# The upper MLP layer of two passes by seven block products of eight, with the weights' block sums made on the side

## The chip, the cores and the metric

The kernel runs on one core of one Trainium2 chip. The metric is the device time of one execution in microseconds (us). The engines are named as in the profile: PE (TensorE matmuls) with PEld (its weight loads), DVE (VectorE), ACT (ScalarE), POOL (GpSimd) and SP (SyncE, which here issues most DMAs).

## The reference

One encoder layer on 2048 tokens of 1024 features, one batch. What matters here is the last third of it:

```python
h = h + concat([att, conv], -1) @ w_out          # mixing: attention and convolution
h = h + cross_attention(rmsnorm(h, norm_x_g)) @ w_xo
u = rmsnorm(h, norm_mlp_g[l]) @ w_up[l]          # 1024 -> 4096, the upper layer
h = h + jnp.square(jax.nn.relu(u)) @ w_down[l]   # 4096 -> 1024, the lower layer
return rmsnorm(h, norm_final_g)
```

Attention is a sliding window at three dilations (8 heads of 64), the convolution has 31 taps over 512 channels. All in float32.

## The kernel before

**Arithmetic.** Every float32 operand of a large product is split into a high and a low float16 part (`split_to`, or an ACT cast and a DVE subtraction), and each product is three matmuls, high by high, high by low, low by high (`mm3`, L370 to L372). A 128x128 block of weights is loaded for every matmul and up to 512 tokens stream past it; sums collect in a PSUM bank of 512 columns.

**Passes.** After the first linear layers the tokens are worked off in four passes `p` of 512 tokens each (`post(p)`). A pass first applies `w_out` (`resid_linear`, tiles `o`), then cross attention (scores `xs`, softmax, output tiles `x` by a second `resid_linear`), then the MLP. Activations are kept with features on the partitions: `hs[m]` is a tile of 128 features by 512 tokens, m from 0 to 7. `resid_linear` makes `hs[m]` on DVE, multiplies it by the norm's gain and splits it into `y["h", m]` and `y["l", m]` (names `mh`, `ml` for the MLP), and adds its square to `ssum`. The norm's factor per token is applied after the product, at the eviction of the upper layer (`rsb`).

**MLP of the first three passes.** The 4096 hidden features are eight groups `fg` of four tiles `c`. For two groups at a time the hidden tiles are made one after the other (tile `up`, 24 matmuls each; then DVE L1601, ACT square L1602, ACT cast L1604, DVE subtraction L1605 give `hhh` and `hhl`), and then eight output tiles (`dn`, 24 matmuls each) add the lower layer's share to `hs[m]` (DVE L1620). Both kinds take turns in three PSUM banks, `mm=(0, 1, 2)`. The lower layer's product runs over the eight hidden tiles in order, k from 0 to 7.

**Weights.** The first pass loads float32 weights, splits them (L357 on ACT, L358 on DVE) and saves the float16 pairs to DRAM tiles `wst`, 512 KB each. The later passes load `wst` again, through a ring of seven tiles (`wtile`, `wpost`). The last pass has its own MLP (`last_mlp`), which already makes its lower layer by seven block products.

**Order of the work.** Python generators yield after each piece. `weave(main, *sides)` runs the pass's generator and, at each of its yields (a main step), lets the side generators advance at a given rate; beside pass p run the attention of pass p+1 (`att`, 0.95) and its convolution (`conv`, 0.85, from main step 23 on in the second and third pass). A convolution step is four DVE instructions on `cacc` (L387). The second pass has 8 steps for `w_out`, 8 for the scores, 11 for the cross attention's output, and 16 for each pair of groups. This is the order in which instructions are written; a list scheduler then fixes each engine's own order by estimated times, taking what stands first and is ready. `issue_after` queues an instruction behind another one of the same engine. Within an engine the order is then fixed. All the weights' DMAs go through SP's queue, in order.

`load_cat` fills the four tiles of the pool `cat0` with the next pass's mixed features late in the MLP, at the last pair of groups.

Of the kernel before, what the change touches and what calls it, by code (L numbers as in the profile page):

```python
# [10 lines left out]
F32 = mybir.dt.float32  # L11
# [10 lines left out]
P = 128  # L22
# [26 lines left out]
def hybrid_layer(ctx, tc, A, out):  # L49
# [69 lines left out]
    wst = [dr.tile([P, 2 * 1024], F16, name=f"wst{i}") for i in range(64)]  # L119
    vscr = dr.tile([P, 2, 8, 256], F16, name="vscr")  # L120
# [25 lines left out]
    gxm = cst.tile([P, 16], F32, name="gxm")  # L146
# [5 lines left out]
    cst.tile([P, 64], F32, name="cpad")  # L152
# [101 lines left out]
    def bounds():  # L254
# [9 lines left out]
        with ExitStack() as st:  # L264
# [13 lines left out]
            TT(c[19], c[0], g2m, op=ALU.mult)  # L278
        yield
# [10 lines left out]
        with ExitStack() as st:  # L290
# [13 lines left out]
            TS(gxm[:, 8:16], gv[:, 16:24], TM, None, op0=ALU.mult)  # L304
        yield
# [1113 lines left out]
    banks.update(mm=(0, 1, 2), O=(7,))  # L1419
# [5 lines left out]
    cv = pool("conv")  # L1425

    def tmp(name, bufs=4, dtype=F32, shape=(P, 512)):
        return pp.tile(list(shape), dtype, tag="tmp", name=name, bufs=bufs)
# [44 lines left out]
    def resid_linear(load, rhs, korder, resid, hs, ssum, scale, gains, y, name, steps=False, wide=False):  # L1473


        for ms in ((0, 1, 2, 3) if wide else (0, 1, 2), () if wide else (3,), (4,), (5,), (6,), (7,)):
# [3 lines left out]
            for ks in [korder[a:b] for a, b in zip(cuts, cuts[1:])] if len(ms) > 1 else (korder,):  # L1480
                for m, (wh, wl) in zip(ms, wt):
# [6 lines left out]
                    if ks[-1] == korder[-1]:  # L1488
# [3 lines left out]
                        ACT.activation(y["h", m], h, AF.Copy, scale=g)  # L1492
                        DVE.scalar_tensor_tensor(y["l", m], h, g, y["h", m], op0=ALU.mult, op1=ALU.subtract)  # L1493
                        add_sq(h, ssum, m == 0)
                        yield

    def post(p):
# [48 lines left out]
        for hp in range(XH // 2):  # L1546
# [4 lines left out]
            for kk in range(4):  # L1551
                ah, al = wpost(ascr[hp, :, 2 * kk:2 * kk + 2, :], f"a{p}{hp}{kk}", S_A, (P, 2, 512))
                for t in range(4):
# [8 lines left out]
                    if kk == 3:  # L1562
# [4 lines left out]
        y = ytiles("m")  # L1567
        ssum = ssum_tile(f"x{p}")
        xl = resid_linear(lambda m: wpost(bscr[m], f"b{p}{m}", S_B), pr_, list(range(KC)), lambda m: hs[m], hs, ssum, K_B,
                          gxm[:, 8:16], y, f"x{p}_", True)  # L1570
# [4 lines left out]
        yield from xl  # L1575
        r = rstd_from(ssum)
        rb = ps("c", "nrb")
        bcast_rows(rb, r, 4)
        rsb = ssum
# [7 lines left out]
        for g in range(FG // 2):  # L1587
            end = g == FG // 2 - 1
            hh = {}
            for fg in (2 * g, 2 * g + 1):  # L1590
                for q in "hl":
                    t = xquad(q, fg % 2, f"hh{q}{p}_{fg}")
                    for j in range(4):
                        hh[q, 4 * (fg % 2) + j] = t[:, j]
                for c in range(4):
                    wh, wl = wpost(wcols(w_up, fg * 512 + c * P), f"u{p}{fg}_{c}", S_UP, (P, 8, P), 4 * fg + c, p)
                    pt = ps("mm", "up")
                    for k in range(KC):
                        mm3(pt, wh[:, k, :], wl[:, k, :], y["h", k], y["l", k], k == 0, k == KC - 1)
# [3 lines left out]
                    j = 4 * (fg % 2) + c  # L1603
# [6 lines left out]
            for mp2 in range(4):  # L1610
                ws = [wpost(wcols(w_down, mp2 * 256, 256, (4 * fg, 4 * fg + 4)), f"d{p}{fg}_{mp2}", S_DN, (P, 4, 256),
                            32 + 4 * fg + mp2, p) for fg in (2 * g, 2 * g + 1)]
                for e in range(2):
# [3 lines left out]
                    for k in range(8):  # L1617
                        wh, wl = ws[k // 4]
                        mm3(pt, wh[:, k % 4, es], wl[:, k % 4, es], hh["h", k], hh["l", k], k == 0, k == 7)
# [178 lines left out]
    for p in range(NG):  # L1798
# [8 lines left out]
        if p + 1 < NG:  # L1807
            cg = conv(cv, p + 1)
            sides = [(att(p + 1), 0.95), (cg, 0.85)]
            weave(islice(main, 23 if p else 14), sides[0])  # L1810
# [60 lines left out]
```

## Time and profile before

| | |
|---|---|
| median of 3 runs | 2701.93 us (2701.36 to 2705.62) |
| profiled execution | 2703.95 us, of which the span from first to last instruction is 2702.1 us |
| instructions | 40538 |
| granted PE clock, mean | 0.994 |
| HBM | 342.52 MB read, 102.12 MB written, 165 GB/s over the span |
| DMA issues of 512 KB for the MLP | `ws_u<-wst` 96, `ws_d<-wst` 64 |

The page gives each engine's busy time, its share of the span in 40 slices, the chain of work that ended last, and the costliest groups of instructions by line, with the mean duration of one and the idle time ahead of them. Views of the trace give the same for a stretch of time, and the waits of an engine with what ended them. Durations of neighbouring instructions on an engine overlap, so that the distance between their starts is the price of one in a stream.

### The profile page before, as it was taken

How to read it: one execution, taken by the hardware profiler on the slowest of the kernel's cores; microseconds unless marked ns; L12 is line 12 of the kernel's file. 1: busy time of each engine (PE TensorE's matmuls, PEld its weight loads, DVE VectorE, ACT ScalarE, POOL GpSimd, SP SyncE). 2: the span in 40 equal slices, each digit the busy share in tenths (PEclk: the TensorE clock that was granted, in tenths of full speed). 3: DMA queues.
4: the chain of work that ended last, by engine and by line, in shares of the span. 5: the costliest groups of instructions: out<-in, count | busy, mean ns of one | idle time of the engine just before them, and what ended most of it. 6: DMA issues, size and time to landing. Idle time of an engine off the chain costs nothing.

```text
span 2702.1 us, 40538 instructions
## 1 busy us (share of the span) xinstructions
PE 2643.7 (98%) x15514; PEld 1447.3 (54%) x15514; DVE 1842.6 (68%) x3565; ACT 1141.9 (42%) x2029; POOL 228.6 (8%) x285
## 2 busy tenths in 40 slices
PE   7989999999899999999999999999999999999998
PEld 7844448777454555445555554455555545444443
DVE  5887656567679996556676763467776435668886
ACT  5737544476454345334531222244221323434433
POOL 1234002032002011100000000000000000000000
PEclk9999999999999999999999999999999999999999
DMA  8977978665635777864344545344445445223231
GB/s 261 300 259 215 285 225 268 171 182 172 169 90 165 235 221 221 259 190 147 113 128 129 147 126 169 123 122 126 135 118 150 148 125 164 94 94 102 89 121 63
DMA packets 396322, 447.31 MB, mean 166 GB/s; under 512 B 87549, under 2 KB 302513, under 8 KB 395360
## 3 DMA queue, kind: packets, MB, share of 16 engines
q1 hardware_dynamic: 388720, 429.70, 53.1%
q10 hardware_dynamic: 5184, 9.01, 0.9%
q0 software_dynamic: 2224, 6.01, 0.6%
q8 instruction: 122, 2.00, 0.3%
q14 instruction: 72, 0.59, 0.1%
HBM read 342.52 MB, written 102.12 MB: 165 GB/s over the span
## 4 chain that ended last, share of the span: by engine, by line
PE 85%; DVE 5%; DMA 5%; ACT 2%; issue 2%; SPq 1%; POOL 0%; DVEq 0%; POOLq 0%; ACTq 0%
PE up L370 8%; PE up L371 8%; PE up L372 8%; PE dn L371 8%; PE dn L370 8%; PE dn L372 8%; PE lin L372 3%; PE lin L371 3%; PE lin L370 3%; PE pt L1026 2%; PE xs L371 2%; PE xs L372 2%; PE o L372 2%; PE xs L370 2%; PE o L370 2%; PE o L371 2%
## 5 line engine op out<-in xcount | busy, mean ns | idle before, releaser
L371 PE MATMUL up<-ml,ws_u 128*128 128x512 f16 x1024 | 388.6, 380 | 0.9 <-DVE ml L1493 0.9
L370 PE MATMUL up<-mh,ws_u 128*128 128x512 f16 x1024 | 388.4, 380 | 0.8 <-DMA ws_u<-wst 0.8
L372 PE MATMUL up<-mh,ws_u 128*128 128x512 f16 x1024 | 387.9, 379 | 0.0
L387 DVE SCALAR_TENSOR_TENSOR cacc<-cu,cw,cacc 128x512 f32<-128x512 f32 x480 | 366.8, 765 | 7.6
L370 PE MATMUL dn<-hhh,ws_d 128*128 128x512 f16 x768 | 290.7, 379 | 0.4 <-ACT hhh L1604 0.4
L371 PE MATMUL dn<-hhl,ws_d 128*128 128x512 f16 x768 | 290.7, 379 | 0.3 <-DVE hhl L1605 0.3
L372 PE MATMUL dn<-hhh,ws_d 128*128 128x512 f16 x768 | 290.7, 379 | 0.0
L1029 ACT CAST ph<-pt 128x512 f16<-128x512 f32 x160 | 91.8, 575 | 217.5 <-PE pt L1026 217.4
L1019 DVE CUSTOM_DVE_ANT_0 sm<-s,mask,qks 128x256 f32<-128x256 f32 (+1 forms) x384 | 150.8, 435 | 46.1 <-PE s L1237 31.5
L1620 DVE SCALAR_TENSOR_TENSOR h<-dn,bd,h 128x512 f32<-128x512 f32 x96 | 71.9, 750 | 152.8 <-PE dn L372 151.2
L372 PEld LDWEIGHTS <-ws_u 128*128 128x128 f16 x1024 | 100.5, 98 | 121.6 <-issue 1.9
L1020 ACT ACTIVATE sm<-sm,o 128x256 f32<-128x256 f32 (+1 forms) x288 | 117.2, 453 | 114.1 <-DVE o L1019 113.7
L370 PEld LDWEIGHTS <-ws_u 128*128 128x128 f16 x1024 | 100.4, 98 | 114.1 <-DMA ws_u<-wst 1.7
L371 PEld LDWEIGHTS <-ws_u 128*128 128x128 f16 x1024 | 100.3, 98 | 112.4 <-issue 0.6
L1030 DVE TENSOR_TENSOR pl<-pt,ph 128x512 f16<-128x512 f32 x160 | 109.9, 687 | 42.7 <-ACT ph L1029 42.5
L1602 ACT ACTIVATE rl<-rl 128x512 f32<-128x512 f32 x96 | 60.0, 627 | 164.0 <-DVE rl L1601 163.8
L1601 DVE SCALAR_TENSOR_TENSOR rl<-up,ssumx 128x512 f32<-128x512 f32 x96 | 65.8, 689 | 92.7 <-PE up L372 91.3
L372 PEld LDWEIGHTS <-ws_d 128*128 128x128 f16 x768 | 75.1, 98 | 90.5 <-issue 0.4
L370 PEld LDWEIGHTS <-ws_d 128*128 128x128 f16 x768 | 75.5, 98 | 83.0
L371 PEld LDWEIGHTS <-ws_d 128*128 128x128 f16 x768 | 75.1, 98 | 83.1
L1026 PE MATMUL pt<-ident,sm 128*128 128x128 f32 x640 | 98.4, 275 | 6.4 <-ACT sm L1020 3.3
L372 PE MATMUL o<-cath,ws_o 128*128 128x512 f16 x256 | 97.7, 383 | 4.3 <-DVE ws_o L358 4.3
(499 smaller groups left out, 6123.9 us busy)
## 6 DMA issues: line engine op xcount, KB each, us to landing
ws_u<-wst SPq DMA_DIRECT2D x96, 512.0 KB
ws_d<-wst SPq DMA_DIRECT2D x64, 512.0 KB
raw_d<-in_w_down_dram SPq DMA_DIRECT2D x36, 512.0 KB
scan<-in_w_up_dram SPq DMA_DIRECT2D x32, 512.0 KB
scan<-in_w_down_dram SPq DMA_DIRECT2D x32, 512.0 KB
raw_o<-in_w_out_dram SPq DMA_DIRECT2D x32, 512.0 KB
raw_a<-ascr SPq DMA_DIRECT2D x32, 512.0 KB
raw_b<-bscr SPq DMA_DIRECT2D x32, 512.0 KB
```

Of the source, the lines that this page charges most:

```text
L370: PE.matmul(o, lh, rh, start=first, stop=False, skip_group_check=more)
L371: PE.matmul(o, lh, rl, start=False, stop=False, skip_group_check=more)
L372: last["pe"] = PE.matmul(o, ll, rh, start=False, stop=end, skip_group_check=more)
L387: DVE.scalar_tensor_tensor(acc, u[:, t:t + 512], cw[:, c, t:t + 1], acc, op0=ALU.mult, op1=ALU.add)
L1019: last["dve"] = DVE.tensor_tensor_reduce(dst, so, mask[:, 256 * m:256 * m + nk], SCORE, 3e38, ALU.add, ALU.min, mn)
L1020: last["act"] = ACT.activation(dst, dst, AF.Exp, bias=mn, scale=-1.0)
L1026: last["pe"] = PE.transpose(pt[:, j, :], sm[:, j, :], ident)
L1029: ACT.copy(ph, pt)
L1030: DVE.tensor_tensor(pl, pt, ph, op=ALU.subtract)
L1601: last["dve"] = DVE.scalar_tensor_tensor(r, pt, 0.0, rsb, op0=ALU.max, op1=ALU.mult)
L1602: ACT.activation(r, r, AF.Square)
L1620: last["dve"] = DVE.scalar_tensor_tensor(hs[m], pt, K_DN, hs[m], op0=ALU.mult, op1=ALU.add)
```

## The change

In the second and third pass (p = 1 and 2) the upper layer of a group `fg` is no longer four tiles of 24 matmuls with 512 columns. The product is taken as 2x2 blocks: the weights' input features in two halves (k 0 to 3, k 4 to 7), the group's hidden features in two halves of two tiles, and the tokens in two halves of 256. Seven products of blocks with sums of blocks replace the eight (`quad`): each is 24 matmuls of 256 columns. Three PSUM banks X, Y and Z hold partial sums; `kept` copies a bank to SBUF by ACT, `done` adds a bank to such a copy on DVE and makes the hidden tiles.

The sums of the activations' blocks (`B11`, `T1`, `T4`, `B2`, `T32`, and `B12` in the second pass) are made where `hs[m]` is made (`put_columns`, in place of the plain split). The sums of the weights' blocks are made by a new side generator (`prep`), twelve steps for a group: it loads the float32 weights into the `cat0` tiles, adds blocks on DVE, splits on ACT and DVE, and stores seven tiles of 512 KB a group to new DRAM tiles `ust`. In the second pass it runs at rate 1.0 from main step 8 on and prepares groups 3 to 7, in the third at 0.6 for groups 0, 1 and 2. So the second pass uses `quad` for groups 3 to 7 only, and makes groups 0 to 2 from the old weights, in two halves of 256 tokens; the third uses it for all eight, in the order 3 to 7, 0 to 2, and issues the first step of its first quad ahead of the norm's sums (`opened`). After quads the lower layer takes k in the order 0, 1, 2, 3, 6, 7, 4, 5. The scale bounds get factors 4 and 16, and `tmp` a fifth buffer. The first and the last pass keep their way.

```diff
@@ buffers and bounds
+    ust = [[dr.tile([P, 2 * 1024], F16, name=f"ust{fg}_{i}") for i in range(7)] for fg in range(8)]
...
+            TS(c[0], c[0], 4.0, None, op0=ALU.mult)
+            TS(c[18], c[18], 16.0, None, op0=ALU.mult)
...
+            TS(gxm[:, 16:24], gxm[:, 8:16], -1.0, None, op0=ALU.mult)
...
-    banks.update(mm=(0, 1, 2), O=(7,))
+    banks.update(mm=(0, 1, 2), ux=(0,), uy=(1,), uz=(2,), O=(7,))
...
-    def tmp(name, bufs=4, dtype=F32, shape=(P, 512)):
+    sw = pool("sums")
+    def tmp(name, bufs=5, dtype=F32, shape=(P, 512)):
@@ resid_linear
-                        ACT.activation(y["h", m], h, AF.Copy, scale=g)
-                        DVE.scalar_tensor_tensor(y["l", m], h, g, y["h", m], op0=ALU.mult, op1=ALU.subtract)
+                        if put:
+                            put(m, h, g)
+                        else:
+                            ACT.activation(y["h", m], h, AF.Copy, scale=g)
+                            DVE.scalar_tensor_tensor(y["l", m], h, g, y["h", m], op0=ALU.mult, op1=ALU.subtract)
@@ new
+    def prep(fgs):
+        late = []
+        def give(d, t):
+            late.append((d, t))
+        def step():
+            for d, t in late:
+                dma(d, t)
+            late.clear()
+        def hi(o, i):
+            ACT.activation(o, i, AF.Copy, scale=S_UP)
+        def lo(o, i, h):
+            DVE.scalar_tensor_tensor(o, i, S_UP, h, op0=ALU.mult, op1=ALU.subtract)
+        for fg in fgs:
+            for j in range(2):
+                nm = f"{fg}{j}"
+                raw = [ct0.tile([P, 8, P], F32, tag=f"ch{i}", name=f"pw{i}_{nm}") for i in range(2)]
+                step()
+                for i in range(2):
+                    dma(raw[i], wcols(w_up, (4 * fg + 2 * i + j) * P))
+                a11, a12, a21, a22 = (r[:, 4 * i:4 * i + 4] for r in raw for i in range(2))
+                yield
+                step()
+                t0 = ct0.tile([P, 2, 8, P], F16, tag="cl0", name=f"pt0_{nm}")
+                hi(t0[:, 0], raw[0])
+                s1 = sw.tile([P, 4, P], F32, tag="s1", name=f"ps1_{nm}")
+                DVE.tensor_tensor(s1, a21, a22, op=ALU.add)
+                DVE.tensor_tensor(a21, a11, a21, op=ALU.subtract)
+                yield
+                step()
+                lo(t0[:, 1], raw[0], t0[:, 0])
+                give(ust[fg][j], flat(t0))
+                DVE.tensor_tensor(a11, s1, a11, op=ALU.subtract)
+                t2 = ct0.tile([P, 2, 8, P], F16, tag="cl1", name=f"pt2_{nm}")
+                hi(t2[:, 0], raw[1])
+                yield
+                step()
+                DVE.tensor_tensor(a12, a12, a11, op=ALU.subtract)
+                lo(t2[:, 1], raw[1], t2[:, 0])
+                give(ust[fg][4 + j], flat(t2))
+                yield
...
+                hi(t1[:, 0, 0:4], a11)
+                hi(t1[:, 0, 4:8], s1)
+                hi(t3[:, 0], a12)
+                yield
+                step()
+                lo(t1[:, 1, 0:4], a11, t1[:, 0, 0:4])
+                lo(t1[:, 1, 4:8], s1, t1[:, 0, 4:8])
+                lo(t3[:, 1], a12, t3[:, 0])
...
+                yield
+            step()
+            ready.add(fg)
+        step()
+    preps = {1: (3, 4, 5, 6, 7), 2: (0, 1, 2)}
...
+        def put(m, h, g):
+            k = m % 4
+            if m < 4:
+                t = tmp("t1")[:, 0:256]
+                DVE.tensor_tensor(t, h[:, 256:512], h[:, 0:256], op=ALU.subtract)
+                for n, x in (("B11", h[:, 0:256]), ("T1", t), ("B12", h[:, 256:512])):
+                    if (n, "h") not in one:
+                        continue
+                    ACT.activation(one[n, "h"][:, k], x, AF.Copy, scale=g)
+                    DVE.scalar_tensor_tensor(one[n, "l"][:, k], x, g, one[n, "h"][:, k], op0=ALU.mult, op1=ALU.subtract)
+                return
+            v, t = tmp("yv"), tmp("t32")
+            ACT.activation(v, h, AF.Copy, scale=g)
+            DVE.scalar_tensor_tensor(t[:, 0:256], hs[k][:, 256:512], gxm[:, 16 + k:17 + k], v[:, 256:512], op0=ALU.mult, op1=ALU.add)
+            DVE.scalar_tensor_tensor(t[:, 256:512], hs[k][:, 0:256], gxm[:, 8 + k:9 + k], t[:, 0:256], op0=ALU.mult, op1=ALU.add)
+            for n, x in (("B2", v), ("T32", t)):
+                a, b = (two_[n, q][k // 2][:, :, k % 2] for q in "hl")
+                ACT.copy(a, halved(x))
+                DVE.tensor_tensor(b, halved(x), a, op=ALU.subtract)
+            DVE.tensor_tensor(v[:, 0:256], v[:, 0:256], t[:, 256:512], op=ALU.subtract)
+            a, b = (one["T4", q][:, k] for q in "hl")
+            ACT.copy(a, v[:, 0:256])
+            DVE.tensor_tensor(b, v[:, 0:256], a, op=ALU.subtract)
...
+    def quad(p, fg, src, hh, rsb):
...
+        def kept(pt, n):
+            e = tmp(f"{n}{p}{fg}")
+            ACT.copy(e, pt)
+            return e
+        def done(e, pt, i, z):
+            DVE.tensor_tensor(e, e, pt, op=ALU.add)
+            e3 = halved(e)
+            last["dve"] = DVE.scalar_tensor_tensor(e3, e3, 0.0, rsb[:, 256 * z:256 * z + 256].unsqueeze(1).to_broadcast([P, 2, 256]),
+                                                   op0=ALU.max, op1=ALU.mult)
+            ACT.activation(e, e, AF.Square)
+            a, b = (t[:, 2 * i:2 * i + 2, 256 * z:256 * z + 256] for t in hh)
+            ACT.copy(a, e3)
+            DVE.tensor_tensor(b, e3, a, op=ALU.subtract)
+        X, Y, Z = (ps(f"u{x}", "up") for x in "xyz")
+        w11, w12 = pair(0)
+        prod(X, w11, "B11")
+        e1 = kept(X, "e1")
+        prod(Y, w12, "B21")
+        yield
+        w2, w1 = pair(2)
+        done(e1, Y, 0, 0)
+        prod(X, w2, "T2", True)
+        e2 = kept(X, "e2")
+        prod(Z, w1, "T1")
+        e4 = kept(Z, "e4")
+        yield
+        w3, w22 = pair(4)
+        prod(X, w3, "T3", True)
+        e3 = kept(X, "e3")
+        done(e4, X, 1, 1)
+        Y = ps("uy", "up")
+        prod(Y, w22, "T4")
+        yield
+        t = tile(6)
+        done(e3, Y, 1, 0)
+        prod(Z, [[t[:, e, 4 * j:4 * j + 4] for e in range(2)] for j in range(2)], "B22", True)
+        done(e2, Z, 0, 1)
+        yield
@@ the passes
-            sides = [(att(p + 1), 0.95), (cg, 0.85)]
-            weave(islice(main, 23 if p else 14), sides[0])
+            sides = [(att(p + 1), 0.95)]
+            prepping[p] = prep(preps.get(p, ()))
+            if p:
+                weave(islice(main, 8), *sides)
+                sides.append((prepping[p], 1.0 if p == 1 else 0.6))
+            weave(islice(main, 15 if p else 14), *sides)
+            sides.append((cg, 0.85))
         weave(main, *sides)
```

92 lines of the change are left out of this document (77 added, 15 removed).

## The prediction

> **What bounds the kernel now.** I read the page first, then the busy times by stretch for the second and third pass, then the waits, then single timelines for the distance between neighbouring instructions.
>
> ```profile
> span 2702.1 us, 40538 instructions
> PE 2643.7 (98%) x15514; PEld 1447.3 (54%) x15514; DVE 1842.6 (68%) x3565; ACT 1141.9 (42%) x2029; POOL 228.6 (8%) x285
> PE 85%; DVE 5%; DMA 5%; ACT 2%; issue 2%; SPq 1%; POOL 0%; DVEq 0%; POOLq 0%; ACTq 0%
> ```
>
> TensorE is the bound: 98% busy, and 85% of the chain that ended last. The stretches of the two passes that change say it more sharply (columns: length, then busy time and instructions of PE, PEld, DVE, ACT, POOL; clock, DMA share, GB/s):
>
> ```profile
> 1377.00:1610.00 233.00, 233.00 (x1365) 120.43 (x1364) 171.82 (x331) 61.32 (x119) 1.20 (x3) 1.00 0.47 132
> 1610.00:1734.00 124.00, 123.34 (x605) 57.69 (x602) 46.00 (x79) 29.05 (x43) 1.01 (x1) 1.00 0.45 137
> 1841.00:1890.00 49.00, 49.00 (x300) 25.70 (x298) 34.65 (x68) 20.57 (x35) 1.38 (x1) 1.00 0.46 139
> 1890.00:2110.00 220.00, 220.00 (x1285) 113.05 (x1284) 163.52 (x316) 56.32 (x110) 1.00 (x2) 1.00 0.46 133
> 2110.00:2250.00 140.00, 140.00 (x706) 67.22 (x705) 56.75 (x99) 34.03 (x51) 2.21 (x3) 1.00 0.45 138
> PE x L370 <- DVE h L1491: 3.1, 1, 3.1
> ```
>
> In the MLP of the second pass (1377 to 1734) and the third (1890 to 2250) PE is busy practically without a gap; the last row is the longest wait of PE in the second pass, and it lies ahead of the MLP. So matmul time taken out there comes off the end, as long as nothing else becomes late. The candidate is DVE: 171.82 of 233 us (74%) while the next pass's convolution and attention run beside the MLP, and only 46.00 of 124 after them.
>
> **What the matmuls give.** A matmul's price is the distance between starts, not its duration, for they overlap:
>
> ```profile
> 1400.05 0.38 PE L372 MATMUL up<-mh,ws_u 128*128 128x512 f16 x1
> ...
> 1401.99 0.38 PE L372 MATMUL up<-mh,ws_u 128*128 128x512 f16 x1
> 429.73 0.27 PE L371 MATMUL v<-wv,xh 128*128 128x256 f16 x1
> ...
> 432.90 0.27 PE L370 MATMUL v<-wv,xh 128*128 128x256 f16 x1
> 1375.11 0.19 PE L1034 MATMUL opt<-v,ph 128*128 128x65 f16 x1
> ...
> 1375.41 0.20 PE L1035 MATMUL opt<-v,ph 128*128 128x64 f16 x1
> ```
>
> 512 columns: 9 steps in 1.94 us, 0.2156 us each. 256 columns, each with weights of its own: 29 steps in 3.17 us, 0.1093. The 65-column ones: 10 steps in 0.30, 0.03 each, again with weights every time; so weight loads hide behind a 256-column matmul. A group fg of four hidden tiles has 4 x 24 matmuls of 512 columns now: 20.69 us. By seven products it has 7 x 24 of 256: 168 x 0.1093 = 18.36. That is 2.33 us less for each of 13 groups (five in the second pass, eight in the third), 30.3 us. The three groups of the second pass that stay whole run in two halves, 192 x 0.1093 = 20.99, which costs 3 x 0.29 = 0.9. **Net 29.4 us off PE.**
>
> [...]
>
> **What it adds on DVE.** Starts of independent DVE instructions:
>
> ```profile
> 1351.18 1.28 DVE L358 SCALAR_TENSOR_TENSOR ws_b<-raw_b,bd,ws_b 128x1024 f16<-128x1024 f32 x1
> 1352.37 0.75 DVE L1493 SCALAR_TENSOR_TENSOR ml<-h,gxm,mh 128x512 f16<-128x512 f32 x1
> 1353.03 0.68 DVE L1443 TENSOR_TENSOR ssumx<-ssumx,sq 128x512 f32<-128x512 f32 x1
> 1353.63 0.75 DVE L1491 SCALAR_TENSOR_TENSOR h<-x,bd,h 128x512 f32<-128x512 f32 x1
> L1670 DVE TENSOR_TENSOR hql<-rl,hqh 128x256 f16<-128x256 f32 x28 | 11.8, 421 | 3.8 <-ACT hqh L1669 3.5
> L1601 DVE SCALAR_TENSOR_TENSOR rl<-up,ssumx 128x512 f32<-128x512 f32 x24 | 16.5, 689 | 19.4 <-PE up L372 18.3 <-ACT ssumx L1580 1.2
> L1620 DVE SCALAR_TENSOR_TENSOR h<-dn,bd,h 128x512 f32<-128x512 f32 x18 | 13.5, 750 | 25.2 <-PE dn L372 25.1
> L1601 DVE SCALAR_TENSOR_TENSOR rl<-up,ssumx 128x512 f32<-128x512 f32 x23 | 15.9, 690 | 19.0 <-PE up L372 18.9
> L1620 DVE SCALAR_TENSOR_TENSOR h<-dn,bd,h 128x512 f32<-128x512 f32 x16 | 12.0, 750 | 25.1 <-PE dn L372 25.1
> ```
>
> So a 1024-wide split costs 1.19 us of the engine, a 512-wide scaled one 0.66, a 512-wide add 0.60, and a 256-wide one about 0.36 (0.421 less the same overlap). The last four rows are the groups of the two busy stretches: 24 + 18 = 42 main steps (hidden or output tiles) in 233 us, 5.55 us a step with 171.82 / 42 = 4.09 of DVE; in the third pass 39 steps, 5.64 us and 4.19.
>
> Prep for one fg is two rounds of 4 adds, 2 splits of 1024 and 3 of 512: 2 x (2.40 + 2.38 + 1.98) = 13.5 us, in 12 steps: 1.13 a step at rate 1 (second pass), 0.68 at rate 0.6 (third). Each quad adds four 512-wide adds: 0.60 for each of its four steps. Hidden steps stand about 0.26 above the mean of DVE, output steps 0.34 below (two instructions against one).
>
> A whole step's products are 24 x 0.2156 = 5.17 us, so 0.38 of the 5.55 is attention; a quad step takes PE 18.36 / 4 + 0.38 = 4.97. While the convolution runs, DVE needs 4.09 + 0.26 + 0.60 + 1.13 = 6.08 in the second pass and 4.19 + 0.26 + 0.60 + 0.68 = 5.73 in the third. So DVE falls behind by 1.11 and 0.76 a step there. An output step gives back 0.7 to 1.0, as it stays at 5.55. Convolution starts at main step 23 and takes 34 steps at 0.85, so it ends near 63; the MLP begins at step 27 with 16 steps for a pair of groups. That leaves 8 quad steps beside it in the second pass (fg 3; fg 4) and 20 in the third. The pairs after it, at 46.00 of 124, have room.
>
> **Where the lag hurts.** DVE works in order, so the instructions that finish a quad queue behind the convolution and prep steps written ahead of them.
>
> ```profile
> L1605 DVE TENSOR_TENSOR hhl<-rl,hhh 128x512 f16<-128x512 f32 x24 | 16.5, 687 | 1.6 <-ACT hhh L1604 1.2
> L1602 ACT ACTIVATE rl<-rl 128x512 f32<-128x512 f32 x96 | 60.0, 627 | 164.0 <-DVE rl L1601 163.8
> L1604 ACT CAST hhh<-rl 128x512 f16<-128x512 f32 x96 | 58.5, 614 | 1.9
> L1491 DVE SCALAR_TENSOR_TENSOR h<-x,bd,h 128x512 f32<-128x512 f32 x32 | 24.0, 749 | 23.5 <-PE x L372 23.5
> L1492 ACT ACTIVATE mh<-h,gxm 128x512 f16<-128x512 f32 x32 | 23.0, 719 | 32.1 <-DVE h L1491 32.0
> ```
>
> From the last product to a usable hidden tile it is 0.69 + 0.63 + 0.61 + 0.69 = 2.62 us now, covered by 21 matmuls of the lower layer (4.53 us). After: one add more, 3.31, and the order 0-3, 6, 7, 4, 5 covers it with 18 matmuls, 3.88. So the slack shrinks from 1.9 to about 0.5 us, and lag beyond that is PE idle. Second pass: 4 x 1.11 - 0.5 = 3.9 once (the second time four steps without convolution make it good). Third: 8 x 0.76 - 0.5 = 5.6 twice. Sum 15.1.
>
> The same ahead of the MLP: for rows m of 4 and above, put_columns replaces one 512-wide split by two adds and two splits of 512 and 256 and two 256-wide adds, 4 x 0.36 + 2 x 0.60 - 0.66 = 2.0 us more. In 1841 to 1890 (8 of these and 2 hidden steps) DVE has 3.47 a step of 5.55; with prep it becomes 6.1 in the third pass and 6.6 in the second, four steps each: lag 2.3 and 4.2. The chain of the last row grows from 0.75 + 0.72 + 0.75 to 0.75 + 0.72 + 0.61 + 0.69 = 2.8; the whole groups of the second pass cover it with 21 half matmuls, 2.3 us (4.53 now), the opened quad of the third with 3.6. PE idle: 4.7 and 1.5. Together 21.3.
>
> The nearest row for a full DVE is the first pass, where weights are split beside the same work:
>
> ```profile
> 860.00:900.00 40.00, 37.80 (x204) 18.86 (x205) 39.93 (x67) 21.40 (x35) 7.88 (x7) 0.91 0.70 206
> 900.00:940.00 40.00, 40.00 (x228) 20.05 (x227) 36.81 (x55) 11.57 (x15) 0.00 (x0) 1.00 0.81 239
> 940.00:980.00 40.00, 40.00 (x242) 20.57 (x241) 38.61 (x61) 19.08 (x30) 12.25 (x12) 1.00 0.69 210
> ```
>
> With DVE at 39.93 of 40 PE loses 2.2 us, at 38.61 nothing. 28 quad steps and 8 residual ones are 183 us; at 2.2 in 40 that is 10.1 us. Bounds 0 (as at 940) and 21.3; I take 16, midway between the two reckonings, since bank reuse is tighter than in the first pass.
>
> **The rest.** ACT gains per prepped fg 4 wide and 6 narrow casts and four copies per quad:
>
> ```profile
> L357 ACT ACTIVATE ws_u<-raw_u,bd 128x1024 f16<-128x1024 f32 x32 | 36.7, 1147 | 72.3 <-PE up L372 30.3 <-PE dn L372 21.1 <-DMA raw_u<-in_w_up_dram 12.6
> ws_u<-wst SPq DMA_DIRECT2D x96, 512.0 KB
> SPq L58 <- DVE ws_d L358: 75.5, 22, 7.3
> 1373.11 0.15 DVE L339 TENSOR_SCALAR st_v<-nps 128x4 f32<-128x4 f32 x1
> ```
>
> 4 x 1.15 + 6 x 0.72 = 8.9 us in 12 steps, 0.74, and 0.6: with 61.32 / 42 = 1.46 now it stays near 2.8 of 5: covered, not free if DVE is late. SP issues per prepped fg 4 loads and 8 stores, and per quad 7 loads for 4. A store waits for DVE's low part and holds the weight loads behind it, as in the first pass (75.5 us in 22 waits, PE still full at 900 to 980); seven tiles are held, one quad ahead, about 20 us. I cost it at 0, and at some 5 us if that cover goes. Bytes in 1377 to 1610: 30.8 MB now, plus 3.3 fg x 5.8 and 3 x 1.6, is 55 MB, 240 GB/s; 900 to 940 carried 239 with PE full. [...] The scale constants are three small DVE instructions (0.15 each by the last row), nothing. Freed banks and one more tmp buffer: nothing by themselves.
>
> **Sum.** 2703.95 (profiled execution, span 2702.1 and 1.85 around it) - 29.4 + 16 = 2690.5; the median shown is 2.0 lower, so 2688.5.
>
> **Rivals.**
> - The lag is absorbed (0 to 5 us lost), as at 940 to 980: 2672 to 2678. For it: conv and prep carry no deadline inside the stretch. Against: quads wait on DVE within one or two products.
> - Slower: one product lasts 24 x 0.1093 = 2.6 us, and X is needed again after one product, X and Y after two. A convolution step is four 0.75 us instructions, 3.0 us. If one such step stands between product and eviction in every quad, PE loses 3 us x 13 = 39, and 6 ahead of the MLP: 29.4 - 45 = 16 slower, 2718. It decides from (29.4 - 6) / 13 = 1.8 us lost per group. For it: DVE at 74% before anything is added. Against: six of the thirteen groups lie after the convolution, where DVE is at 37 to 40%.
> - DMA is late: at 206 GB/s (860 to 900) 55 MB take 267 us for 233: 2730.
> [...]
> - It evens out within 0.2%: waits of 24 to 35 us.
>
> **Chances.** Forecast as told (waits of 9 to 24 us, 2682 to 2696) 0.36; absorbed 0.21; even 0.15; slower by lag 0.21; DMA 0.06; weight loads 0.01. A measurement of this kernel tells about 0.2% (5.4 us) from no change: faster 0.57, same 0.15, slower 0.28. The range 2671 to 2719 leaves out DMA, weight loads and the upper part of the lag.
>
> **What would show it.** Right: 0.109 between 256-column matmuls of the quads; DVE at 95% or more in both stretches; PE waits on hh low parts at the start of the lower layer of the pairs beside the convolution, and on the last B2 or T32 part. Wrong: PE without gaps (absorbed); PE waiting on ACT or DVE inside every quad, also late in the pass (slower); waits on ust loads (DMA); a pitch over 0.12.

## The result and the profile after

The changed kernel takes 2748.88 us (median, 2748.12 to 2750.49) against 2701.64 us (2701.24 to 2705.62): 1.0172 times as long, 95% interval 1.0155 to 1.0190. That is 47 us slower. The prediction was 2688.5 us, faster, in a range of 2671 to 2719.

The page's first lines after, in the order of the ones shown of before (span, busy times, chain by engine, and here the chain by line):

```profile
span 2746.4 us, 43761 instructions
PE 2643.4 (96%) x16738; PEld 1578.6 (57%) x16738; DVE 1993.2 (73%) x3824; ACT 1250.1 (46%) x2197; POOL 227.9 (8%) x285
PE 77%; DVE 9%; DMA 8%; issue 2%; ACT 2%; SPq 1%; POOL 0%; DVEq 0%; POOLq 0%; ACTq 0%
PE dn L376 8%; PE dn L375 8%; PE dn L374 8%; PE up L375 7%; PE up L374 7%; PE up L376 7%; PE lin L376 3%; PE lin L374 3%; PE lin L375 3%; DMA pw<-in_w_up_dram 3%; PE pt L1030 2%; PE o L374 2%; PE o L376 2%; PE o L375 2%; PE s L1241 1%
```

PE's share of the chain falls from 85% to 77%, and a name that did not exist before stands in it: `pw<-in_w_up_dram`, the loads of `prep`. PE's busy total is as large as before although it has less to do; part of what it does runs slower, as the next view shows.

The same stretches of the second pass (scores; cross attention's output; first pair's upper layer; rest of the MLP) and of the third (the first three together; the rest), before and after. Columns as in the prediction: length, busy time of PE, PEld, DVE, ACT, POOL; granted clock, DMA share, GB/s.

```profile
1254.00:1310.00 56.00, 55.75 (x341) 29.93 (x339) 36.08 (x82) 27.56 (x56) 2.20 (x2) 1.00 0.41 116
1310.00:1364.00 54.00, 50.52 (x294) 26.32 (x292) 33.59 (x67) 26.30 (x51) 0.00 (x0) 0.97 0.44 132
1364.00:1412.00 48.00, 48.00 (x290) 25.36 (x287) 41.41 (x86) 15.76 (x30) 1.51 (x2) 1.00 0.36 103
1412.00:1727.00 315.00, 315.00 (x1731) 156.84 (x1730) 183.19 (x346) 74.96 (x135) 1.71 (x3) 1.00 0.46 134
1775.00:1922.00 147.00, 146.91 (x879) 78.24 (x878) 103.93 (x223) 65.19 (x127) 4.22 (x4) 1.00 0.39 112
1922.00:2239.00 317.00, 317.00 (x1755) 158.58 (x1754) 188.69 (x352) 78.19 (x138) 1.71 (x3) 1.00 0.46 137
```

```profile
1251.00:1320.00 69.00, 61.99 (x338) 31.63 (x337) 53.52 (x104) 38.35 (x68) 2.58 (x2) 0.90 0.71 215
1320.00:1380.00 60.00, 44.68 (x259) 24.64 (x258) 48.99 (x99) 35.28 (x65) 0.00 (x0) 0.89 0.75 225
1380.00:1456.00 76.00, 66.03 (x518) 51.08 (x516) 68.76 (x133) 37.63 (x65) 1.52 (x2) 0.86 0.64 203
1456.00:1759.00 303.00, 303.00 (x2184) 201.04 (x2183) 210.36 (x388) 93.76 (x164) 1.71 (x3) 1.00 0.59 181
1807.00:1980.00 173.00, 154.66 (x1019) 96.45 (x1017) 150.37 (x304) 99.76 (x180) 4.06 (x4) 0.91 0.69 212
1980.00:2282.00 302.00, 302.00 (x2182) 199.91 (x2181) 204.65 (x384) 91.92 (x163) 1.41 (x3) 1.00 0.57 175
```

Read the fourth and the last row of each first: where most of the quads are, the stretches become shorter (315.4 to 303.4 and 315.4 to 302.0 us, counted between the stages' first matmuls), and PE has no gap. The loss lies ahead of that, in the cross attention and the upper layer of the first pair of groups: 158 us become 205 in the second pass, 147 become 173 in the third. PE idles there for 7.0 + 15.3 + 10.0 + 18.3 = 50.6 us, and its clock falls to a mean of 0.86 to 0.91. `prep` was expected to run from the scores deep into the MLP; the tile view of its inputs says where it ran (first and last start in the second pass):

```profile
L1518 ACT ACTIVATE pt<-pw,bd x40: 705/928/1167, 1263.6 to 1476.6; 128x1024 f16<-128x1024 f32 x20, 128x512 f16<-128x512 f32 x20
L1521 DVE SCALAR_TENSOR_TENSOR pt<-pw,bd,pt x40: 700/1012/1286, 1264.7 to 1480.0; 128x1024 f16<-128x1024 f32 x20, 128x512 f16<-128x512 f32 x20
```

All five groups were worked off in 216 us, 1264 to 1480, beside the cross attention and the first pair of groups. Its 60 steps are written over 60 main steps, up to the middle of the MLP.

What that did, in one place. PE and then DVE in the timeline (start, length; in brackets the idle time before and its releaser):

```profile
1328.72 0.27 PE L1241 MATMUL s<-k,ql 128*128 128x256 f16 x1
1333.34 0.37 PE L1241 MATMUL s<-k,qh 128*128 128x256 f16 x1 [4.36 <-DVE o L1023]
...
1325.23 0.62 DVE L1711 TENSOR_SCALAR xp<-xp,xdn 128x256 f32<-128x256 f32 x2
1329.96 0.69 DVE L1537 TENSOR_TENSOR pw<-pw,pw 128x512 f32<-128x512 f32 x1 [4.11 <-DMA pw<-in_w_up_dram]
1331.20 1.28 DVE L1521 SCALAR_TENSOR_TENSOR pt<-pw,bd,pt 128x1024 f16<-128x1024 f32 x1 [0.55 <-ACT pt L1518]
1332.40 0.48 DVE L1023 CUSTOM_DVE_ANT_0 sm<-s,mask,qks 128x256 f32<-128x256 f32 x1
...
1405.56 0.41 DVE L1613 TENSOR_TENSOR T4l<-yv,T4h 128x256 f16<-128x256 f32 x1
1405.90 0.74 DVE L1521 SCALAR_TENSOR_TENSOR pt<-ps,bd,pt 128x512 f16<-128x512 f32 x1
1406.56 0.68 DVE L1547 TENSOR_TENSOR pw<-pw 128x512 f32<-128x512 f32 x1
1407.16 0.74 DVE L1521 SCALAR_TENSOR_TENSOR pt<-pw,bd,pt 128x512 f16<-128x512 f32 x1
1407.82 0.68 DVE L1609 TENSOR_TENSOR B2l<-yv,B2h 128x512 f16<-128x512 f32 x1
```

The window attention's scores were ready at 1329. DVE stood idle, 4.11 us, with a subtraction of `prep` at its head that waited for a weight load, then did another instruction of `prep`, and only then the `sm` step that PE needed; PE idled 4.36 us. At 1406 the other form: nothing is waited for, but three instructions of `prep` (2 us) stand ahead of the `B2l` that the next matmul needs. The waits of 1251 to 1456 (engine, line, what was waited for: total, times, longest) are of both forms:

```profile
ACT pt L1518 <- DMA pw<-in_w_up_dram: 29.9, 6, 9.8
ACT pt L1518 <- DMA ust<-pt: 13.3, 7, 5.6
DVE pw L1537 <- DMA pw<-in_w_up_dram: 12.9, 5, 4.1
PE x L374 <- ACT ws_b L361: 5.5, 1, 5.5
PE up L375 <- DVE B2l L1609: 5.1, 2, 3.3
PE s L1241 <- DVE o L1023: 4.4, 1, 4.4
```

ACT stood 43 us and DVE 13 us with one of `prep`'s instructions at the head of the queue and everything else behind it. All 32.3 us that PE idles in these 205 us end with a result of ACT or DVE.

### The profile page after: what moved, and what is told of

The parts are those of the page before. It is cut to its first block, busy times and chain, and to the rows that moved or that the text cites. A ratio compares the mean times of both kernels' runs of the same rounds, so it can differ in the third digit from the quotient of the medians.

```text
span 2746.4 us, 43761 instructions
## 1 busy us (share of the span) xinstructions
PE 2643.4 (96%) x16738; PEld 1578.6 (57%) x16738; DVE 1993.2 (73%) x3824; ACT 1250.1 (46%) x2197; POOL 227.9 (8%) x285
## 4 chain that ended last, share of the span: by engine, by line
PE 77%; DVE 9%; DMA 8%; issue 2%; ACT 2%; SPq 1%; POOL 0%; DVEq 0%; POOLq 0%; ACTq 0%
PE dn L376 8%; PE dn L375 8%; PE dn L374 8%; PE up L375 7%; PE up L374 7%; PE up L376 7%; PE lin L376 3%; PE lin L374 3%; PE lin L375 3%; DMA pw<-in_w_up_dram 3%; PE pt L1030 2%; PE o L374 2%; PE o L376 2%; PE o L375 2%; PE s L1241 1%
## 5 line engine op out<-in xcount | busy, mean ns | idle before, releaser
L375 PE MATMUL up<-ml,ws_u 128*128 128x512 f16 x512 | 194.0, 379 | 1.0 <-DVE ml L1501 1.0
L374 PE MATMUL up<-mh,ws_u 128*128 128x512 f16 x512 | 193.5, 379 | 1.3 <-DMA ws_u<-wst 1.3
L376 PE MATMUL up<-mh,ws_u 128*128 128x512 f16 x512 | 193.7, 379 | 0.0
L376 PEld LDWEIGHTS <-ws_u 128*128 128x128 f16 x704 | 69.8, 99 | 69.6 <-issue 6.7
L374 PEld LDWEIGHTS <-ws_u 128*128 128x128 f16 x704 | 69.8, 99 | 66.0 <-issue 3.3
L374 PE MATMUL x<-pth,ws_b 128*128 128x512 f16 x256 | 98.1, 389 | 9.4 <-ACT ws_b L361 5.5
L375 PEld LDWEIGHTS <-ws_u 128*128 128x128 f16 x704 | 69.7, 99 | 60.6 <-issue 0.3
L347 POOL TENSOR_TENSOR nr<-st_v,mhalf 128x4 f32<-128x4 f32 (+1 forms) x15 | 14.9, 991 | 1063.3 <-DVE st_v L343 1062.7
L374 PE MATMUL xs<-ws_a,yh 128*128 128x512 f16 x256 | 98.0, 390 | 5.2 <-ACT xp L1707 3.5
```

The costliest lines, as they stand in the source:

```text
L347: POOL.tensor_tensor(dst, v, mhalf.to_broadcast([P, v.shape[1]]), op=ALU.pow)
L374: PE.matmul(o, lh, rh, start=first, stop=False, skip_group_check=more)
L375: PE.matmul(o, lh, rl, start=False, stop=False, skip_group_check=more)
L376: last["pe"] = PE.matmul(o, ll, rh, start=False, stop=end, skip_group_check=more)
```

## The experiments

Each ratio below is to the kernel before, run on the same chip, with its 95% interval; "against before" is the difference of the two medians. The theory after the profile: the matmuls' gain is real, and `prep` costs more than it, because the scheduler, which takes what is ready, pulls its instructions ahead of short chains that PE waits for. The rivals: the quads or `put_columns` cost as well; DVE and ACT have no room; the transfers are the loss. In e1, e6, e7, e9 and e11 to e14 the quads read plain weights in place of the sums, so these kernels give times and not the layer's values.

**Without prep, and prep alone.** e1 leaves `prep` out:

```diff
-    preps = {1: (3, 4, 5, 6, 7), 2: (0, 1, 2)}
+    preps = {1: (), 2: ()}
-            dma(flat(t), ust[fg][i])
+            dma(flat(t), wst[(4 * fg + i) % 32])
-                if src and (fg in ready or fg in preps[p]):
+                if src and (p == 2 or fg > 2):
```

> The changed kernel without the weights' block sums: nothing is prepared, and the quads read seven saved tiles of 512 KB of the plain upper weights instead of the sums, so the matmuls, copies and loads are the same and the hidden values are not the layer's. Theory A (the loss is prep's work run beside the cross attention, whose DVE and ACT queues it fills and blocks): the second pass's scores, residual layer and first pair go back to about their length before, and with 29.4 us off PE and a few us for put_columns the kernel takes 2675 to 2685. Theory B (the loss is put_columns and the halves of the whole groups): those stages stay long, 2725 or more. My predicted mechanism (lag at the start of the lower layer) expects 2678 or so, too, but the trace shows no wait there.

Measured: 2669.7 us, ratio 0.9880 (0.9866 to 0.9895), 32.3 us below before. All waits of PE in 1207 to 2300 that the view lists:

```profile
PE dn L374 <- DMA ws_d<-wst: 0.4, 1, 0.4
PE s L1241 <- DVE o L1023: 0.3, 1, 0.3
```

So quads, `put_columns`, the halves and seven loads a quad cost nothing that shows. The time is 5 us under the span of theory A.

e2 keeps `prep` and takes the upper layer as before:

```diff
-        if p in preps:
+        if False:
             one, two_, src = columns(p)
-        order = (3, 4, 5, 6, 7, 0, 1, 2) if p == 2 else range(8)
+        order = range(8)
-        if p == 2:
+        if False:
             opened = hidden_tiles(0, order[0])
```

> Only the weights' block sums are made and stored beside the second and third pass; both passes keep the plain upper layer and the plain split, so nothing reads the sums. Theory A: the loss stays without the gain, 2755 to 2775. Theory B: prep hides beside a PE that is the bound, 2702 to 2712.

Measured: 2759.31 us, ratio 1.0218 (1.0202 to 1.0233), 57.3 us above before. Nothing but `prep` is added here, and the loss lies in the same two stretches (190 and 171 us, where before has 158 and 147).

**Its place and its order.** e3 queues each of `prep`'s DVE and ACT instructions behind the pass's last one (`pinned`, which the kernel has for other side work); e4 writes `prep` only from the MLP on; e5 does both:

```diff
@@ e3, e5
-            prepping[p] = prep(preps.get(p, ()))
+            prepping[p] = pinned(prep(preps.get(p, ())), "dve", "act")
@@ e4, e5
-            if p:
-                weave(islice(main, 8), *sides)
-                sides.append((prepping[p], 1.0 if p == 1 else 0.6))
-            weave(islice(main, 15 if p else 14), *sides)
+            weave(islice(main, 23 if p else 14), *sides)
             sides.append((cg, 0.85))
+            if p:
+                weave(islice(main, 4), *sides)
+                sides.append((prepping[p], 1.2 if p == 1 else 0.8))
```

> The changed kernel with each prep step's DVE and ACT instructions queued behind the last instruction that the pass and the attention have issued on that engine, so that the scheduler cannot move them far ahead of their place. Theory A': the loss comes from prep being run earlier than its rate says (all 20 loads of the second pass are issued by 1480 us, where the rate asks for some 12): with it held back, a good part of the 47 us returns, 2690 to 2715, and now the lag that I predicted in the MLP may show. Rival: the prep that belongs beside the cross attention by its own rate does the harm: 2735 to 2750.

> The changed kernel with prep begun at main step 27 (the MLP) instead of 8, at 1.2 and 0.8 a step. Theory A (prep beside the cross attention is what costs): most of the loss goes, 2685 to 2705, with some waits in the MLP's first two pairs, where DVE now has convolution, attention and prep. Rival (prep costs its engine time wherever it lies): 2735 or more.

> Both edits of the two runs before at once: prep begins at main step 27 (the MLP) at 1.2 and 0.8 a step, and its DVE and ACT instructions are queued behind the last ones of the pass and the attention. Begun late without the queueing, its first load still went out at 1262 us, long before the MLP, so the begin in the program alone did not move it. Theory A' (prep harms where it meets the cross attention, and only queueing keeps it away): the scores and residual stages go back to within a few us of their length without prep, and the kernel takes 2672 to 2688. Rival (my predicted lag, now that convolution, attention, prep and quads meet in the MLP): waits on hhh and hhl at the start of the lower layer return what is won, 2695 to 2710.

Measured: e3 2698.48 us, ratio 0.9991 (0.9981 to 1.0002); e4 2747.8, 1.0172 (1.0157 to 1.0188); e5 2697.73, 0.9979 (0.9970 to 0.9987). The tile view of the inputs, second pass, e4 and then e3:

```profile
L1518 ACT ACTIVATE pt<-pw,bd x40: 705/933/1157, 1267.0 to 1480.8; 128x1024 f16<-128x1024 f32 x20, 128x512 f16<-128x512 f32 x20
```

```profile
L1518 ACT ACTIVATE pt<-pw,bd x40: 705/928/1149, 1263.9 to 1611.0; 128x1024 f16<-128x1024 f32 x20, 128x512 f16<-128x512 f32 x20
```

Written 19 main steps later, `prep` still began at 1267 us and ended at 1481: the place in the program does not move it. So e4's time is in its rival's span, but does not test the rival, since `prep` did not change its place. Queued behind the pass's instructions, it ran to 1611 as written, and 50 us came back. Only both together keep it out of the cross attention: from the scores to the end of the first pair's upper layer e5 takes 154 and 141 us, as e1 does, and e3 178 and 148. Yet e5 is no faster than e3, for the rest of the second pass's MLP takes 327 us in e5, 308 in e3 and 303 in e1. So e5's theory was right on the stages and missed the time, which is in the rival's span; but PE's waits are not the ones that the rival named. The largest part is for the copies `e` that free the quads' banks (9.5 us), and 0.4 us is for `hhl`.

**Work or transfers.** e6 keeps the engines' work of `prep` and drops nearly all its transfers; e7 keeps the transfers and drops the work:

```diff
@@ e6: one pair of tiles loaded per pass, nothing stored, quads from wst
-                raw = [ct0.tile([P, 8, P], F32, tag=f"ch{i}", name=f"pw{i}_{nm}") for i in range(2)]
+                if not keep:
+                    keep.extend(ct0.tile([P, 8, P], F32, tag=f"ch{i}", name=f"pw{i}_{nm}") for i in range(2))
+                raw = keep
-            late.append((d, t))
+            return
@@ e7: loads as they are, the same bytes stored from one tile, quads from wst
-                hi(t0[:, 0], raw[0])
-                DVE.tensor_tensor(s1, a21, a22, op=ALU.add)
...
-                give(ust[fg][j], flat(t0))
+                give(ust[fg][j], flat16(raw[0]))
```

> The changed kernel with prep's DVE and ACT instructions at their places, but on one pair of weight tiles loaded once a pass, with no further loads and no stores (subtractions are made maxima and minima so that values stay bounded); the quads read saved plain weights, as in the run without prep. If the loss (79 us between the changed kernel and the one without prep) is waiting for prep's DMAs at the head of the DVE and ACT queues, this takes 2670 to 2685; if it is the engine time and the order of prep's instructions, 2720 to 2750.

> The changed kernel with prep's DMAs alone: the same loads of upper weights, and as many stores of as many bytes (from a tile that is loaded once), no DVE or ACT work in prep; the quads read saved plain weights. If the traffic or the place in SP's queue is what costs, this takes 2720 or more; if DMAs cost only where DVE or ACT wait for them, 2668 to 2680.

Measured: e6 2730.69 us, ratio 1.0106 (1.0090 to 1.0122), 27.3 above before; e7 2696.48, 0.9976 (0.9967 to 0.9985), 6.9 below. Against e1's 32.3 below, the work alone costs 60 us and the transfers alone 25 us. e6 is in the span of engine time and order; e7 is in neither of its spans. PE's largest waits are for `xp` of the softmax (9.0 us) in e6 and for `ws_b` and `ws_a`, the cross attention's weights whose loads came late (9.1 and 4.9 us), in e7. Both causes are real; the work is the larger. But neither ran at the pace that it has in the changed kernel, so these are not exact shares of its loss. With no loads to wait for, e6's work of the second pass ran from 1270 to 1406 us, in 136 us instead of 216; with no work to wait for, e7's 20 loads and 40 stores were issued from 1258 to 1389, with 340 GB/s at a DMA share of 0.97 in 1249 to 1315.

**What stays when it is queued late.** e5 still stands 27 us above e1. e8 loads three steps ahead instead of one, ahead of the stores (rates 1.6 and 1.1); e10 also moves one group from the second pass to the third, at rates 1.2 and 1.4:

```diff
@@ e8, e10
-                step()
                 for i in range(2):
                     dma(raw[i], wcols(w_up, (4 * fg + 2 * i + j) * P))
+                step()
                 yield
-                step()
+                yield
+                yield
@@ e10
-    preps = {1: (3, 4, 5, 6, 7), 2: (0, 1, 2)}
+    preps = {1: (4, 5, 6, 7), 2: (0, 1, 2, 3)}
-        order = (3, 4, 5, 6, 7, 0, 1, 2) if p == 2 else range(8)
+        order = (4, 5, 6, 7, 0, 1, 2, 3) if p == 2 else range(8)
```

> Block sums queued behind the passes' own instructions and begun at main step 27, as in e5, but each pair of weight tiles is loaded three side steps ahead of its first use instead of one, and its loads are issued ahead of the waiting stores (rates 1.6 and 1.1, since each half now has two steps more). Theory that e5's loss of 28 us against e1 is mostly VectorE and ScalarE standing in line behind a block-sum instruction that waits for its load: the lower and upper layers of the second pass lose their gaps, 2676 to 2690 us. Rival, that what is left is the transfers themselves (e7, with transfers alone, stood 27 us above e1 as well): 2694 to 2700 us, as e5.

> As e8, but with four groups' sums made beside each pass (4 to 7 beside the second, 0 to 3 beside the third) in place of five and three, so that the second pass has four groups by seven products and not five. TensorE does about 2.4 us more (one pair with one group of seven products, 44.3 against 46.9 us), and the second pass loses a fifth of the sums' instructions and transfers. Theory (waiting at the head of the queues): 2 us above e8 if e8 has no gaps left, and below it by up to 5 us if e8 still has gaps in the second pass. Rival (transfers set it): below e8 by a fifth of what the second pass still loses, 2 to 4 us.

Measured: e8 2695.49 us, ratio 0.9974 (0.9963 to 0.9986); e10 2719.43, 1.0064 (1.0051 to 1.0078). e8's time is its rival's. In 1365 to 1740 ACT and DVE wait 23.6 us for `prep`'s loads, where e5 has 74.3; but ACT waits 17.9 us for stores that still hold the result tiles, where e5 has 8.1, and nothing was won that is clear of the intervals. e8 changes the lead, the order of loads and stores and the rates at once, and does not part them. e10 is in neither of its spans and says little on the question. At its rate (64 steps at 1.2, 53 main steps) group 7 is finished just as its quad begins, and PE waits for it:

```profile
PE up L374 <- DMA ws_t<-ust: 12.2, 3, 9.0
PE up L374 <- ACT e L1637: 6.8, 1, 6.8
```

So e8 is the fastest complete version, 0.26% below before and not surely below e5.

The late place was then taken apart. e9 is e6 pinned and in its early place; e11 is e6 and e12 is e7 in the place of e5; e13 is e5 without the stores, e14 e11 with them:

```diff
@@ e9: e6 with        prepping[p] = pinned(prep(preps.get(p, ())), "dve", "act")
@@ e11, e12: e6, e7 with that and the weave lines of e5
@@ e13: e5 with quads from wst and
-            late.append((d, t))
+            return
@@ e14: e11 with
-            return
+            late.append((d, t))
```

> As e6 (the sums' VectorE and ScalarE work alone: one pair of tiles loaded per pass, nothing stored, differences taken as max and min, so that the values are not the weights' sums; the seven products read the ordinary weight tiles), but with that work queued behind the pass's own instructions. Theory that the order harms and not the engines' time: 2670 to 2682 us, within 12 us of e1's 2669.7. Rival, that VectorE and ScalarE have no room for 130 us of work beside these stages: over 2700 us, near e6's 2730.7.

> As e9 (work alone, queued behind the pass's instructions, one pair of tiles loaded per pass, nothing stored, differences as max and min, products from the ordinary weight tiles), but begun at main step 27 as in e5. Theory that VectorE and ScalarE have room for the sums beside the upper and lower layers and not beside the cross attention and the first pair, where e9 lost all of its 23 us: 2669 to 2676 us. Rival, that e5's remaining 28 us above e1 are these engines' time in any place: 2688 to 2698 us.

> As e7 (the sums' transfers alone: the same loads, and the same bytes stored from a tile as it was loaded; products from the ordinary weight tiles), but begun at main step 27 as in e5. Theory that e5's remaining loss needs both, engines' work that waits in line for late loads: transfers alone cost little here, 2669 to 2680 us. Rival, that the transfers delay the pass's own weight tiles: 2688 to 2698 us.

> e5 without the stores of the sums: loads and engines' work as in e5, nothing stored, the products read the ordinary weight tiles. Theory that VectorE and ScalarE stand in line behind loads that come late: 2688 to 2696 us, most of e5's 28 us stays. Rival, that the loads come late because they stand behind the stores in the queue, or that the bytes of both together delay the pass's weight tiles: 2672 to 2682 us.

> e5 without the loads of the sums' inputs: one pair of tiles loaded per pass (differences as max and min, so that the values stay bounded and are not the weights' sums), engines' work and stores as in e5, the products read the ordinary weight tiles. Theory of the late loads: 2672 to 2680 us. Rival, stores or bytes: 2682 to 2696 us.

| kernel | prep's parts | us | ratio (interval) | against before |
|---|---|---|---|---|
| e1 | none | 2669.70 | 0.9880 (0.9866 to 0.9895) | -32.3 |
| e9 | work, queued, early | 2692.31 | 0.9966 (0.9954 to 0.9978) | -9.4 |
| e11 | work, queued, late | 2672.33 | 0.9884 (0.9871 to 0.9898) | -30.0 |
| e14 | work and stores, queued, late | 2680.35 | 0.9914 (0.9901 to 0.9928) | -24.1 |
| e13 | work and loads, queued, late | 2686.47 | 0.9941 (0.9929 to 0.9953) | -18.0 |
| e5 | all, queued, late | 2697.73 | 0.9979 (0.9970 to 0.9987) | -5.6 |
| e12 | transfers, late | 2700.96 | 0.9995 (0.9984 to 1.0005) | -1.4 |

e9 and e11 part cleanly. Even in written order the work costs 23 us when it begins beside the scores; begun with the MLP it costs 2. e9 lies between the spans of its theory and its rival; e11's theory holds. In the late place stores add 6 us, loads 12, both 24. That is 6 us above their sum, about what the intervals of four ratios leave open, so it is not shown that each makes the other worse. Neither the theory's nor the rival's span held e13 (2686.5 lies between 2682 and 2688), and e14, at 2680.35, lies just above its theory's. e12's theory missed, for a reason that its windows show, and it does not price the transfers in the late place: with no work to pace them, they ran ahead into the cross attention (DMA share 0.82), as in e7:

```profile
1310.00:1420.00 110.00, 91.25 (x645) 58.12 (x642) 78.05 (x171) 52.35 (x102) 1.87 (x2) 0.94 0.82 252
1420.00:1520.00 100.00, 100.00 (x800) 72.16 (x798) 75.00 (x138) 22.65 (x43) 0.00 (x0) 1.00 0.47 139
```

What e5's rest is, one stretch of the second pass's MLP shows. e11, and then e5 with ACT's and DVE's waits in 1365 to 1740:

```profile
1485.00:1620.00 135.00, 135.00 (x1039) 93.51 (x1037) 132.02 (x252) 61.90 (x107) 0.64 (x2) 1.00 0.58 170
```

```profile
1485.00:1620.00 135.00, 128.24 (x980) 88.81 (x979) 123.06 (x235) 56.95 (x101) 0.64 (x2) 0.99 0.81 253
```

```profile
ACT pt L1518 <- DMA pw<-in_w_up_dram: 54.6, 9, 15.9
DVE pw L1537 <- DMA pw<-in_w_up_dram: 19.7, 6, 5.9
```

DVE is busier in e11 (98%) and PE full. In e5 DVE does less, its queue held by loads that have not come, and PE loses 6.8 us. So it is not the amount of work. The last pair's upper layer loses as much again (PE busy for 40.49 of the 48 us from 1649; 37.19 of the 38 us from 1640 in e11). Waiting for loads need not be all of it, as e8 shows: which of loads, stores and their order in SP's queue sets e5's rest stays open.

## Why the prediction was wrong

**The matmuls: right.** 29.4 us were predicted, and e1 gives 32.3 (28 to 36 by its interval). From the MLP's first matmul to the next pass's `w_out` e1 takes 11.7 us less in the second pass and 19.0 less in the third, 30.7 together, where 10.8 and 18.6 were forecast. Some 4 us more lie ahead of the second pass's MLP, in a wait and a piece at a lower clock (0.97 in 1310 to 1364) that before has and e1 has not; the forecast did not count on them. The distance in a quad of the changed kernel:

```profile
1600.47 0.27 PE L374 MATMUL up<-T1h,ws_t 128*128 128x256 f16 x1
...
1602.98 0.27 PE L376 MATMUL up<-T1h,ws_t 128*128 128x256 f16 x1
```

23 steps in 2.51 us, 0.1091 each with a weight load every time, against 0.1093 taken. That is 0.0013 above half of a 512-column step (0.1078), so the weight loads, to which the prediction gave a chance of 0.01, are not the loss.

**DVE's lag beside the MLP: over-sized.** The queue reckoning gave 15.1 us at the lower layer and 21.3 in all. e1 has DVE's added work of `put_columns` and quads and no lag; e11 has that of `prep` beside the MLP too, and loses 2 us with DVE at 132.02 of 135. The reckoning let convolution and `prep` keep their written pace and the quad's finish fall behind. The rival "absorbed" described this stretch rightly: side work without a deadline gave way. In the second pass the convolution's last step starts at 1595 us in e11 and at 1570 in e1.

**The step that failed: the cost and the place of `prep`.** This is the step that turned a forecast gain into a loss, and it has three parts.
- It was costed where it is written to run beside the MLP, at 1.13 and 0.68 us of DVE a step. Ahead of the MLP it was counted for four steps of the residual layer (part of 4.7 and 1.5 us), and beside the scores not at all. Measured there: 21 us in the second pass and 7 in the third with the work in written order (e9, 174.8 and 148.4 us from the scores to the end of the first pair's upper layer, e1 153.8 and 141.3), and 51 and 32 as the kernel is (204.8 and 173.1; all counted between the first matmuls of the stages). DVE at 64% and 62% in the two stretches of the cross attention before looked like room. But PE's listed waits there, 3.6 us in all, end with DVE. One reading added to it: the stretch of 1841 to 1890 has 49 us for its ten steps, 4.90 each, and was reckoned at 5.55; at 4.90 the two terms would have been 7.3 and 4.2, still far from what was measured.
- It was taken to run at its written rate. Nothing held it there, as e4 shows: unqueued, it took 216 us instead of the 352 of e3.
- Its DMAs were put at 0, "and at some 5 us if that cover goes". Alone and unpaced they cost 25 us (e7); in the late place, beside the work, they add 24 (e5 against e11). A limit at the 239 GB/s that the kernel before carried in 900 to 940 was not the mechanism: the stretch carried 203 to 225 GB/s, and 239 is no ceiling either, for the changed kernel carried 304 in 1680 to 1700 with PE busy for all 20 us. What the changed kernel's trace shows is order: ACT and DVE wait 42.8 us at the head of their queues for `pw`. In e7, where the pass's `ws_a` and `ws_b` come late, the DMA engines were nearly full as well (share 0.97), and the run does not part the two. The cover named there, seven weight tiles ahead, held in e7 for the MLP's tiles alone: PE's waits list none for them, and 14.0 us for `ws_b` and `ws_a`.

In sum: 32 us won and 80 lost by `prep` (47.2 + 32.3), where 16 were forecast. That work and transfers taken singly come to about the same (60 + 25) is partly chance, since each ran at another pace alone.

**The rivals.** The slower one (2718) put the loss into every quad. The second pass's quads, all after 1456, wait for nothing; in the third pass only the first ones wait, for inputs that come late (`h`, `B2h`, `B2l`: 5.2 us in 1922 to 1980), and none after 1980. "DMA is late" (2730) named a resource that does cost, by another path; its 34 us (267 for 233) on top of 2688.5 would give 2722.5 and not 2730. None held that the side work would be pulled forward.

## What to carry to other kernels

Before new side work is costed, ask what fixes its place: a list scheduler runs it as soon as it is ready, so it must be priced in the most delicate stretch that it can reach, not in the one where it is written. A busy share of 62 to 64% did not mean room here: side instructions of 0.7 to 1.3 us that stood ahead of the matmuls' next operand made TensorE wait. And a side instruction that waited for a load stopped what stood behind it in its engine's queue (DVE stood for 4.11 us, PE for 4.36). Here queueing it behind the main work brought back 50 us, and what its loads and stores still cost ate nearly all that was left of the gain.

## What the runs showed of the clock

The granted clock fell even where PE made no pause over 1.82 us. These are two places of the changed kernel by windows (length, then as above), the second pass's first pair and its scores, and a few matmuls of the first place in the timeline:

```profile
1397.40:1400.80 3.40, 1.20 (x10) 0.78 (x8) 3.10 (x7) 3.40 (x7) 0.00 (x0) 1.00 0.29 117
1400.80:1414.50 13.70, 8.17 (x38) 5.32 (x38) 13.70 (x29) 5.97 (x12) 0.00 (x0) 0.50 0.43 143
1274.50:1277.90 3.40, 1.44 (x10) 0.69 (x8) 3.40 (x6) 2.68 (x4) 1.39 (x1) 1.00 0.54 129
1277.90:1284.80 6.90, 5.93 (x15) 2.03 (x15) 5.18 (x13) 0.91 (x2) 0.00 (x0) 0.51 1.02 358
```

```profile
1399.15 0.49 PE L374 MATMUL up<-B2h,ws_u 128*128 128x256 f16 x3 [1.03 <-ACT B2h L1608]
1401.45 0.37 PE L375 MATMUL up<-B2l,ws_u 128*128 128x256 f16 x1 [1.82 <-DVE B2l L1609]
1401.62 0.42 PE L376 MATMUL up<-B2h,ws_u 128*128 128x256 f16 x1
1401.83 0.42 PE L375 MATMUL up<-B2l,ws_u 128*128 128x256 f16 x1
```

PE was busy for 1.20 of 3.4 us, its longest gap 1.82 us, and for the next 13.7 us it was granted half the clock: 0.21 us between 256-column matmuls, where a quad at full clock has 0.109. From 1274.5, with 1.44 of 3.4 us and no gap over 1.74, half the clock followed for 6.9 us; from 1349.6, with 2.05 of 3.4 us, it stayed at 1.00. In the two bad stretches the clock stood at half for 79 us in all, in pieces of 3.4 to 13.7 us; before it was one piece of 3.4. So the 50.6 us of idle PE cost some 30 us more in slow matmuls, by an estimate: the two stretches stand 51 and 32 us above e1's, 83 together, with the same matmuls in them. In these rows half the clock followed 3.4 us in which PE was idle for 65% and for 58%, and did not follow 3.4 us in which it was idle for 40%; what decides between these they do not show.
